# Recurrent steps set between attention steps, and a shorter program for the experts' third blocks

## The chip, the cores and the metric

One NeuronCore of a Trainium2 chip runs one layer of a hybrid decoder in a single launch. The measure is the device time of that core in microseconds, lower is better. Engines are named as in the profile: PE (TensorE, matrix products), DVE (VectorE), ACT (ScalarE), POOL (GpSimd) and SP (SyncE, which here issues transfers).

## What is computed

The layer projects 2048 tokens of width 1024 once, and four mixers work on the columns: RWKV (A), gated linear attention (B, "GLA"), mLSTM (C) and latent softmax attention (D). Their outputs are projected and normalized; then a mixture of 32 experts, two for each token, and a gated side input follow.

```python
u  = x @ w_in[i]
ua, ub, uc, ud = split_last(u, (D_IN_A, D_IN_B, D_IN_C, D_IN_D))
ya = rwkv7_group(ua, ...)
yb = gla_group(ub, ...)          # chunked scan: scores in the chunk, plus a carried state
yc = mlstm_group(uc, ...)        # chunked scan with a carried maximum
yd = mla_group(ud, cos, sin, ...)
mix = jnp.concatenate([ya, yb, yc, yd], axis=-1) @ w_out[i]
x   = layer_norm(DN_ALPHA * x + mix, ln1_g[i], ln1_b[i], LN_EPS)
ffn = hier_moe(x, w_rg, b_rg, w_re, b_re, w_gate, w_up, w_down)
ple = jax.nn.sigmoid(x @ ple_w_gate[i] + ple_b_gate[i]) * (p[i] @ ple_w[i])
x   = layer_norm(DN_ALPHA * x + ffn + ple, ln2_g[i], ln2_b[i], LN_EPS)
# an expert: (silu(xb @ w_gate[e]) * (xb @ w_up[e])) @ w_down[e]
```

## The kernel before

The program runs in stages: projections with the RWKV mixer (to about 1060 us), the attention stage (to about 1590), output projection, side input and routing (to about 2016), the experts (to about 3010) and the last normalization.

**Attention stage.** Tokens go in four quarters of 512. Softmax attention is a generator, `d`, of small steps: `mla_attend` makes the scores of one block of 128 keys against 512 queries (three matmuls at L1242 into an `sbank`), their exponential on ACT (`mla_pt`), its sum on POOL or DVE (`mla_acc`, L1248) and now and then the product with the values (`obank`, L1222). Steps of the query maximum are mixed in: a matmul into an `mbank` (L1205), then a reduction `mla_m` on DVE (L1209). The keys and queries are split in a high and a low part, the low ones by DVE at L52 (`mla_kl`, `mla_ql`).

GLA (`gla`) and mLSTM (`mlstm`) go through a quarter in four tiles of 128 tokens. A GLA tile copies the query into the zeroed `gl_qz` (L743), multiplies for scores into a `gbank` (L745), masks them on DVE into `g_am` (L747), transposes the key into another `gbank` (L749, `g_kk`), forms the state's new part (L752), and adds the products of state and scores (`acc`, L264 and L268), copied to `g_yt` by ACT (L767). An mLSTM tile works likewise with `cbank`s and ends in `c_yt` (L967) and the state's update (L975). After the fourth tile of a quarter, `head_norm` (L284 to L294) normalizes the whole quarter, 128 x 1024 elements for each of the two, on DVE, ACT and POOL, and the gate is applied (L776, L981).

The banks (`gbank`, `cbank`, `mbank`, `sbank`, `obank`) are accumulators from small pools: a matmul into a bank waits until the last reader of that buffer is done. A scheduler reorders the emitted instructions on each engine, so the order of an engine is near that of the code but not the same; it is shown below where it matters. In `layer` the loop over 16 tiles emits eight steps of attention (`MLA_RATE`), then a GLA tile and an mLSTM tile.

**Experts.** For each expert the tokens come in blocks of 128, the first always (`moe_gu` 48 matmuls, `moe_dn` 24), the second if the expert has more than 128 tokens, the third if it has more than 256. Counts are known at run time only, so the second and third block stand under an `If` of the program. Each number is split in high and low part, and a product is three passes: high x high, high x low, low x high. For a block of at most 64 tokens `sized` (L1911) picks a shorter program in which the low parts of the tokens stand in the second half of the block's 128 columns ("spread"), so that two passes do. `third(e)` (L1926 to L1943) holds, in one If (L1929), the third block's down product of expert e (L1931) and the gate and up products of expert e+1 (L1936), each with both programs: 4 transposes and 24 + 16 matmuls, 8 transposes and 48 + 32 matmuls, 132 in all. The If of the second block's gate and up products is at L1969, with 48 + 32 matmuls. Products of high and low rows are added by `fold` (gate and up) and in `moe_y` with the mask `half`, L1843 (down).

Of the kernel before, what the change touches and what calls it, by code (L numbers as in the profile page):

```python
# [8 lines left out]
F32 = mybir.dt.float32  # L9
# [21 lines left out]
class Layer:  # L31
# [701 lines left out]
    def gla(self, q):  # L733
        nc, e, s1 = self.nc, self.e, self.s1
        qt, kt, v, gate = self.gin.pop(q)
        fin = self.gfin[:, q]
        yt = e.tile([128, 4, 256], F32, name="g_yt", bufs=1)
        for tt in range(4):
            c = slice(tt * 128, tt * 128 + 128)
            qz = self.qz[tt % 2]  # L740
            for hd in range(4):
                g = slice(32 * hd, 32 * hd + 32)
                nc.vector.tensor_copy(qz[g, hd, :], qt[g, c])  # L743
            p = self.gbank()
            nc.tensor.matmul(p, kt[:, c], qz, start=True, stop=True)  # L745
            st = e.tile([128, 4, 128], F32, name="g_am")
            nc.vector.tensor_mul(st, p.rearrange("p (h i) -> p h i", h=4), self.incl[:, None, :].to_broadcast([128, 4, 128]))  # L747
            p = self.gbank()
            nc.tensor.transpose(p[:, 0:128], kt[:, c], self.ident)  # L749
            kk = e.tile([128, 128], F32, name="g_kk")  # L750
            nc.scalar.copy(kk, p[:, 0:128])
            nc.tensor.matmul(p[:, 256:512], kk, v[:, tt, :], start=True, stop=True)  # L752
            po = self.gbank()
            first = q == 0 and tt == 0
            if not first:
                x = e.tile([128, 256], F32, name="gl_x", bufs=1)
                nc.vector.scalar_tensor_tensor(x, self.gxe, fin[:, tt:tt + 1], self.gbd.rearrange("p h c -> p (h c)"),
                                               op0=OP.mult, op1=OP.mult)
                nc.tensor.matmul(po[:, 0:256], qt[:, c], x, start=True, stop=False, skip_group_check=True)
                nc.vector.tensor_add(self.gxe, p[:, 256:512], x)  # L760
            else:
                self.zero_bank(po, 256)
                nc.vector.tensor_copy(self.gxe, p[:, 256:512])
            for hd in range(4):
                g = slice(64 * hd, 64 * hd + 64)
                self.acc(po[:, g], st[:, hd, :], v[:, tt, g])
            nc.scalar.copy(yt[:, tt, :], po[:, 0:256])  # L767
            if tt == self.LOAD_AT and q < 3:
                self.gla_load(q + 1)
            yield  # L770
        self.gla_out(q, yt, gate)
# [152 lines left out]
    def mlstm(self, q):  # L924
# [3 lines left out]
        for tt in range(4):  # L928
# [9 lines left out]
            for hd in range(4):  # L938
                nc.scalar.activation(w[:, hd], p[:, hd * 128:hd * 128 + 128], AF.Exp, bias=self.mgt[:, 0, 16 * hd + ch:16 * hd + ch + 1])
            pr = e.tile([128, 4, 128], F32, name="c_am")  # L940
            for s in range(2):
                g = slice(64 * s, 64 * s + 64)
                p = self.cbank()
                for hp in range(2):
                    nc.tensor.matmul(p[:, hp * 128:hp * 128 + 128], qk[2 + hp][g, c], qk[hp][g, c], start=True, stop=True)
                nc.vector.scalar_tensor_tensor(pr[:, s::2, :], p[:, 0:256].rearrange("p (a i) -> p a i", a=2), 0.125, w[:, s::2, :],
                                               op0=OP.mult, op1=OP.mult)
            p = self.cbank()
            for hp in range(2):
# [3 lines left out]
                                           g4(2)[:, :, None].to_broadcast([128, 4, 64]), op0=OP.mult, op1=OP.mult)  # L953
            pn = self.cbank()
# [12 lines left out]
            nc.vector.tensor_mul(yt[:, tt, :].rearrange("p (h c) -> p h c", h=4), hn[:, :, 0:64], dn[:, :, None].to_broadcast([128, 4, 64]))  # L967
            pk = self.cbank()
# [10 lines left out]
            yield  # L979
# [713 lines left out]
    def lists(self, lt):  # L1693
# [24 lines left out]

        def pick(j, i):

            nc.vector.tensor_copy(u, p[:, j * 128:j * 128 + n])
            nc.vector.tensor_sub(u, u, p[:, i * 128:i * 128 + n])
            nc.vector.tensor_mul(u, u, half)
            nc.vector.tensor_add(u, u, p[:, i * 128:i * 128 + n])
# [63 lines left out]
    def passes(self, x, wh, wl, k, half):  # L1788
# [4 lines left out]
        return (x[0][:, k], wh), (x[0][:, k], wl), (x[1][:, k], wh)  # L1793

# [57 lines left out]
    def moe(self, G0=(), x0=None, experts=32):  # L1852
# [74 lines left out]
        def third(e):  # L1927

            with tc.If(cnt[e + 1, "four"] > 256):  # L1929
                if e >= 0:  # L1930
                    with tc.If(one(e) > 256):  # L1931
                        h = self.moe_ht(hx, spread=True)
                        sized(e, 2, lambda s: self.moe_dn(h, DW[e], yb, half=s))
                        self.moe_put(self.moe_y(yb, half(e, 2)), put(e, 2))
                if e + 1 < experts:
                    with tc.If(one(e + 1) > 256):  # L1936
                        x = self.turned(X[2], spread=True)
                        sized(e + 1, 2, lambda s: self.moe_gu(x, GW[e + 1], yb, half=s))
# [248 lines left out]
def layer(ctx, tc, I, out):  # L2187
# [3 lines left out]
    with ExitStack() as c:  # L2191
# [35 lines left out]
        for i in range(16):  # L2227
            if i >= L.MLA_WAIT:
                for _ in range(L.MLA_RATE):
                    next(d, None)  # L2230
            next(g)
            next(m)
# [51 lines left out]
```

## Time and profile before

| | us |
|---|---|
| median of 3 runs (3108.67 to 3115.36) | 3111.82 |
| the profiled execution | 3114.34 |
| its span, first to last instruction | 3112.4 |
| PE busy in it | 2830.1 |
| DVE busy | 1949.2 |
| ACT busy | 1224.5 |
| POOL busy | 892.6 |

The granted TensorE clock has a mean of 0.941 over the span. A windows row gives for each engine the busy time and, in brackets, the number of instructions; PEclk is the mean granted clock of that stretch as a share of full speed. A wait is put down to the instruction that released it last.

### The profile page before, as it was taken

The page shows a single profiled execution, that of the slowest core. Times are in us where ns is not written, and L with a number is a line of the kernel's source. Part 1 is how long each engine was busy: PE and PEld are TensorE (multiplying, and loading weights), DVE is VectorE, ACT ScalarE, POOL GpSimd, SP SyncE. Part 2 cuts the span into 40 slices and gives each one's busy share as a digit, 9 for nine tenths or more (in the row PEclk, how much of TensorE's full clock was granted, in tenths as well). Part 3 has the DMA queues.
Part 4 walks back from the last instruction along what each step waited for, and adds up shares of the span by engine and source line. Part 5 has one row for each costly group of instructions (what it writes and reads, how often), then busy time and mean ns, then how long its engine had stood idle before and what let it go on. Part 6 is the DMA issues. An engine that isn't in the chain of part 4 may idle for free. (4 is left out here: it accounts for less than half of the span.)

```text
span 3112.4 us, 42881 instructions
## 1 busy us (share of the span) xinstructions
PE 2830.1 (91%) x15420; PEld 2239.0 (72%) x15421; DVE 1949.2 (63%) x4094; ACT 1224.5 (39%) x2001; POOL 892.6 (29%) x552
## 2 busy tenths in 40 slices
PE   8999999998999899989999999888889988998883
PEld 6888888777877665655567799777667766776662
DVE  6366543566555466667656644676667756666869
ACT  4223232222124332323320122265666756666752
POOL 1000100111010023334331201445454545554525
PEclk9999999999998898979999999999999989999996
DMA  6332143111134522110143412377687867777873
GB/s 186 109 93 75 47 130 93 52 57 56 53 80 136 177 58 70 47 39 18 55 158 136 147 62 75 105 277 257 203 271 242 274 206 233 268 260 224 284 247 137
DMA packets 287055, 443.19 MB, mean 142 GB/s; under 512 B 84088, under 2 KB 152040, under 8 KB 286760
## 3 DMA queue, kind: packets, MB, share of 16 engines
q1 hardware_dynamic: 272200, 397.78, 38.3%
q0 software_dynamic: 14560, 41.47, 5.4%
q8 instruction: 185, 3.03, 0.4%
q14 instruction: 110, 0.90, 0.1%
HBM read 350.52 MB, written 96.50 MB: 144 GB/s over the span
## 5 line engine op out<-in xcount | busy, mean ns | idle before, releaser
L1802 PE MATMUL m_g<-m_g,xhl 128*128 128x512 f32 x2032 | 514.4, 401 | 15.1 <-PEq L1929 9.4
L1802 PEld LDWEIGHTS m_g<-m_g,xhl 128*128 128x128 f32 x2032 | 372.6, 190 | 105.8 <-issue 31.2
L1773 DVE TENSOR_TENSOR m_g<-m_raw,m_g 128x1024 fp32r<-128x1024 f32 x188 | 260.9, 1413 | 131.9 <-ACT m_g L1772 112.5
L1772 ACT CAST m_g<-m_raw 128x1024 fp32r<-128x1024 f32 x252 | 255.3, 1057 | 123.4 <-PEq L1929 110.5
L1834 PE MATMUL m_y<-m_dh,m_h 128*128 128x512 f32 x672 | 239.6, 421 | 24.9 <-PEq L1929 6.5
L59 PE MATMUL pbank<-xh,wh 128*128 128x512 f32 x544 | 220.6, 405 | 10.6 <-DVE us L209 7.7
L60 PE MATMUL pbank<-xl,wh 128*128 128x512 f32 x544 | 219.4, 403 | 0.0
L61 PE MATMUL pbank<-xh,wl 128*128 128x512 f32 x544 | 218.6, 402 | 0.1
L51 ACT CAST xhl<-bank 128x512 fp32r<-128x512 f32 x204 | 118.3, 607 | 251.5 <-PE bank L1350 250.2
L1773 POOL TENSOR_TENSOR m_g<-m_raw,m_g 128x1024 fp32r<-128x1024 f32 x64 | 183.6, 2951 | 88.1 <-ACT m_g L1772 48.3
L1408 PE MATMUL wide<-wt,xhl 128*128 128x512 f32 x768 | 183.5, 398 | 3.6 <-ACT xhl L51 3.6
L1773 POOL TENSOR_TENSOR m_dl<-m_raw,m_dh 128x1024 fp32r<-128x1024 f32 x64 | 178.0, 2806 | 20.6 <-ACT m_dh L1772 20.3
L1834 PEld LDWEIGHTS m_y<-m_dh,m_h 128*128 128x128 f32 x672 | 137.3, 204 | 59.7 <-issue 9.4
L1408 PEld LDWEIGHTS wide<-wt,xhl 128*128 128x128 f32 x768 | 144.1, 189 | 39.8 <-ACT xhl L51 7.3
L1248 POOL TENSOR_TENSOR mla_acc<-mla_acc,mla_pt 128x512 f32<-128x512 f32 (+3 forms) x112 | 137.7, 1230 | 115.0 <-ACT mla_pt L1246 94.5
L52 DVE TENSOR_TENSOR xhl<-bank,xhl 128x512 fp32r<-128x512 f32 x204 | 136.5, 685 | 50.4 <-ACT xhl L51 48.6
L1848 POOL DMA_INDIRECT accd<-m_y,m_put x47 | 92.4, 1967 | 255.1 <-ACT m_y L1841 160.6
L1246 ACT ACTIVATE mla_pt<-sbank 128x512 f32<-128x512 f32 (+3 forms) x160 | 85.0, 532 | 200.6 <-PE sbank L1242 116.8
L1834 PE MATMUL m_y<-m_dl,m_h 128*128 128x512 f32 x376 | 155.8, 414 | 0.0
L1588 PE MATMUL gate<-wt,xhl 128*128 128x354 f32 (+1 forms) x864 | 150.2, 331 | 0.3 <-ACT xhl L51 0.2
L59 PE MATMUL pbank<-wh,xh 128*128 128x256 f32 x512 | 150.3, 294 | 0.0
L60 PE MATMUL pbank<-wl,xh 128*128 128x256 f32 x512 | 150.0, 293 | 0.0
(635 smaller groups left out, 6306.2 us busy)
## 6 DMA issues: line engine op xcount, KB each, us to landing
m_raw<-in_moe_w_down SPq DMA_DIRECT2D x64, 1024.0 KB
m_raw<-in_moe_w_gate SPq DMA_DIRECT2D x126, 512.0 KB
m_raw<-in_moe_w_up SPq DMA_DIRECT2D x126, 512.0 KB
wraw<-in_w_in SPq DMA_DIRECT2D x80, 256.0 KB
o_x<-in_x SPq DMA_DIRECT2D x16, 512.0 KB
x1d<-m_g SPq DMA_DIRECT2D x16, 512.0 KB
accd<-wide SPq DMA_DIRECT2D x16, 512.0 KB
m_raw<-accd SPq DMA_DIRECT2D x7, 1024.0 KB
```

The costliest lines, as they stand in the source:

```text
L51: nc.scalar.copy(hi, src)
L52: (eng and nc.gpsimd or nc.vector).tensor_sub(lo, src, hi.bitcast(F32))
L59: nc.tensor.matmul(out, lh, rh, start=start, stop=False)
L60: nc.tensor.matmul(out, lh, rl, start=False, stop=False)
L61: nc.tensor.matmul(out, ll, rh, start=False, stop=stop)
L1248: (nc.vector if kt in self.SUMS else nc.gpsimd).tensor_add(acc[:, c0 * 128:512], acc[:, c0 * 128:512], pt[:, 0:n])
L1408: nc.tensor.matmul(p[:, j], a[:, k], W[k][bb][:, j * 512:j * 512 + 512], start=k == 0 and i == 0, stop=k == 7 and i == 2)
L1588: nc.tensor.matmul(p[:, 0:n], a[:, k], b[:, o:o + n], start=k == 0 and i == 0, stop=k == 7 and i == 2)
L1772: self.nc.scalar.copy(h[:, i], raw[:, i])
L1773: lo_eng.tensor_sub(l[:, i], raw[:, i], h[:, i].bitcast(F32))
L1802: self.mark["pe"] = self.nc.tensor.matmul(banks[:, j], a, b[:, k % 2, j * 512:j * 512 + 512], start=k == 0 and i == 0, stop=k == 7 and i = ...
L1834: self.nc.tensor.matmul(p[:, j], a, b[:, k % 2, j * 512:j * 512 + 512], start=k == 0 and i == 0, stop=k == 3 and i == len(ps) - 1)
```

## The change

In the attention stage, `gla` and `mlstm` now yield after each small piece, seven times for a GLA tile and eight for an mLSTM tile, and say "tile" at its end. The loop in `layer` takes one step of attention, then one piece of GLA and one of mLSTM, eight times for a tile; what is left of the tile then follows. The addition to the GLA state (`gl_xe`) stands ahead of the product with the old state, and the bank of that product is taken later.

```diff
         for i in range(16):
-            if i >= L.MLA_WAIT:
-                for _ in range(L.MLA_RATE):
-                    next(d, None)
-            next(g)
-            next(m)
+            rest = [g, m]
+            for k in range(L.MLA_RATE):
+                next(d, None)
+                for x in list(rest):
+                    if next(x) == "tile":
+                        rest.remove(x)
+            for x in rest:
+                while next(x) != "tile":
+                    pass
```

In `gla` the piece ends are these (those of `mlstm` are of the same kind: after the weights `ml_w`, after each half of `c_am`, two after `ml_kw`, two after `c_yt`, and "tile"):

```diff
                 nc.vector.tensor_copy(qz[g, hd, :], qt[g, c])
+            yield
             p = self.gbank()
             nc.tensor.matmul(p, kt[:, c], qz, start=True, stop=True)
             st = e.tile([128, 4, 128], F32, name="g_am")
             nc.vector.tensor_mul(st, p.rearrange("p (h i) -> p h i", h=4), self.incl[:, None, :].to_broadcast([128, 4, 128]))
+            yield
+            yield
             p = self.gbank()
             nc.tensor.transpose(p[:, 0:128], kt[:, c], self.ident)
             kk = e.tile([128, 128], F32, name="g_kk")
             nc.scalar.copy(kk, p[:, 0:128])
+            yield
             nc.tensor.matmul(p[:, 256:512], kk, v[:, tt, :], start=True, stop=True)
-            po = self.gbank()
...
+                nc.vector.tensor_add(self.gxe, p[:, 256:512], x)
+                yield
+                yield
+                po = self.gbank()
                 nc.tensor.matmul(po[:, 0:256], qt[:, c], x, start=True, stop=False, skip_group_check=True)
-                nc.vector.tensor_add(self.gxe, p[:, 256:512], x)
...
-            yield
+            yield "tile"
```

In the experts' third blocks one program takes the place of two. `beside_lo` puts the low parts of the first 64 columns beside the high ones, times the mask `half` (one where the block has at most 64 tokens, else zero); `lean` then makes two passes, and a third, low x high, under an If of its own when there are more than 64. The bodies hold 4 + 16 + 8 and 8 + 32 + 16 matmuls, 84 in all. Where blocks are listed, `pick` takes the mask `plain`, which is one for third blocks.

```diff
+    def beside_lo(self, x, m):
+        hi, lo = x[0], x[1]
+        self.nc.vector.scalar_tensor_tensor(hi[:, :, 64:128], lo[:, :, 0:64].bitcast(F32), m, hi[:, :, 64:128].bitcast(F32),
+                                            op0=OP.mult, op1=OP.add)
+
+    def lean(self, x, W, p, n, full):
+        for j in range(2):
+            c = slice(j * 512, j * 512 + 512)
+            for k in range(n):
+                wh, wl = W[k // 2]
+                for i, w in enumerate((wh, wl)):
+                    self.nc.tensor.matmul(p[:, j], x[0][:, k], w[:, k % 2, c], start=k == 0 and i == 0, stop=k == n - 1 and i == 1)
+        with self.tc.If(full):
+            for j in range(2):
+                for k in range(n):
+                    self.acc(p[:, j], x[1][:, k], W[k // 2][0][:, k % 2, j * 512:j * 512 + 512], stop=k == n - 1)
...
                     with tc.If(one(e) > 256):
-                        h = self.moe_ht(hx, spread=True)
-                        sized(e, 2, lambda s: self.moe_dn(h, DW[e], yb, half=s))
+                        h = self.moe_ht(hx)
+                        self.beside_lo(h, half(e, 2))
+                        self.lean(h, DW[e], yb, 4, cnt[e, "pe"] > 320)
...
                     with tc.If(one(e + 1) > 256):
-                        x = self.turned(X[2], spread=True)
-                        sized(e + 1, 2, lambda s: self.moe_gu(x, GW[e + 1], yb, half=s))
+                        x = self.turned(X[2])
+                        self.beside_lo(x, half(e + 1, 2))
+                        self.lean(x, GW[e + 1], yb, 8, cnt[e + 1, "pe"] > 320)
```

Line numbers move: L745 becomes L746, L749 becomes L752, L747 becomes L748, L1242 becomes L1257, L1205 becomes L1220, L1929 becomes L1968.

PE at the end of the attention stage's second quarter, before, from the last attention product to the GLA transpose and a little beyond:

```order
L1222 MATMUL obank<-mla_pt,mla_v_8192 64x384
L745 MATMUL gbank<-gl_qz_8062,g_k 128x512
L933 LDWEIGHTS identb
L933 MATMUL cbank<-negm,identb 128x512
L268 MATMUL cbank<-ml_nmu,ident 128x128 x3
L749 MATMUL gbank<-ident,g_k 128x128
L268 MATMUL cbank<-ml_nmu,ident 128x128
L945 MATMUL cbank<-c_a,c_k 128x128
L752 MATMUL gbank<-g_v,g_kk 128x256
```

PE at the same place now, from the GLA score product on:

```order
L746 MATMUL gbank<-gl_qz_8061,g_k 128x512
L1220 MATMUL mbank<-mla_kh_8188,mla_qh 128x512
L955 MATMUL cbank<-c_a,c_k 128x128
L955 MATMUL cbank<-c_q,c_z 128x128
L1257 MATMUL sbank<-mla_qh,mla_kh_8189 128x512
L1257 MATMUL sbank<-mla_ql,mla_kh_8189 128x512
L1257 MATMUL sbank<-mla_qh,mla_kl_8191 128x512
L1220 MATMUL mbank<-mla_kh_8188,mla_qh 128x256
L268 LDWEIGHTS identb
L268 MATMUL mbank<-negq,identb 128x128
L955 MATMUL cbank<-c_a,c_k 128x128
L1220 MATMUL mbank<-mla_kh_8188,mla_qh 128x512
```

Between the score product and the transpose (L749, now L752, which stands 17 rows after L746) there are now scores and query maxima of two attention steps.

DVE at the end of the first quarter, before, from the first sum of mLSTM's `head_norm` to the mask product:

```order
L284 TENSOR_REDUCE hn_stc_th<-c_yt 128x16
L52 TENSOR_TENSOR mla_kl_8190<-mla_x,mla_kh_8188 64x512
L285 TENSOR_SCALAR hn_stc_th<-hn_stc_th 128x16
L286 TENSOR_TENSOR c_yt<-c_yt,hn_stc_th 128x1024
L52 TENSOR_TENSOR mla_kl_8190<-mla_x,mla_kh_8188 64x512
L52 TENSOR_TENSOR mla_ql<-mla_x,mla_qh 96x512
L747 TENSOR_TENSOR g_am<-gbank,incl 128x512
```

DVE at the same place now:

```order
L284 TENSOR_REDUCE hn_stc_th<-c_yt 128x16
L289 TENSOR_REDUCE hn_stg_th<-g_th 128x16
L990 SCALAR_TENSOR_TENSOR ml_st_8075<-ml_st_8075,ml_dc,cbank 64x65 x2
L990 SCALAR_TENSOR_TENSOR ml_st_8076<-ml_st_8076,ml_dc,cbank 64x65 x2
L290 TENSOR_SCALAR hn_stg_th<-hn_stg_th 128x16
L285 TENSOR_SCALAR hn_stc_th<-hn_stc_th 128x16
L52 TENSOR_TENSOR mla_kl_8190<-mla_x,mla_kh_8188 64x512
L68 TENSOR_SCALAR rs_thg_th<-hn_stg_th 128x16
L286 TENSOR_TENSOR c_yt<-c_yt,hn_stc_th 128x1024
L69 TENSOR_SCALAR hn_rsg_th<-rs_thg_th 128x16
L71 TENSOR_TENSOR rs_thg_th<-hn_rsg_th 128x16
L72 SCALAR_TENSOR_TENSOR rs_thg_th<-rs_thg_th,hn_stg_th 128x16
```

The mask product (now L748) follows right behind; `head_norm` of GLA now runs among that of mLSTM instead of ahead of it, two of the three splits at L52 stand behind the mask product, and the next two reductions of the query maximum come 44 rows after it.

PE in the gate and up part of the third blocks' If, before:

```order
L1943 TENSOR_LOAD m_tcnt
L1936 COMPARE_AND_BRANCH
L1350 MATMUL bank<-ident,m_xg_18063 128x128 x8
L1911 COMPARE_AND_BRANCH
L1802 MATMUL m_y<-m_g,xhl 128x512 x48
L1911 UNCONDITIONAL_BRANCH
L1802 MATMUL m_y<-m_g,xhl 128x512 x32
L1911 UNCONDITIONAL_BRANCH
L1936 UNCONDITIONAL_BRANCH x2
L1929 UNCONDITIONAL_BRANCH
```

PE in the same part now:

```order
L1984 TENSOR_LOAD m_tcnt
L1976 COMPARE_AND_BRANCH
L1365 MATMUL bank<-ident,m_xg_18066 128x128 x8
L1828 MATMUL m_y<-m_g,xhl 128x512 x32
L1829 COMPARE_AND_BRANCH
L268 MATMUL m_y<-m_g,xhl 128x512 x16
L1829 UNCONDITIONAL_BRANCH x2
L1976 UNCONDITIONAL_BRANCH x2
L1968 UNCONDITIONAL_BRANCH
```

The choice between 48 and 32 matmuls has become 32 always and 16 more under an If.

## Rows read from the trace of the kernel before

**Rows 1.** The page: engines' busy time, share and instructions.

```profile
PE 2830.1 (91%) x15420; PEld 2239.0 (72%) x15421; DVE 1949.2 (63%) x4094; ACT 1224.5 (39%) x2001; POOL 892.6 (29%) x552
```

**Rows 2.** Windows: stretch, its length, each engine's busy us, clock, DMA, GB/s.

```profile
1060.00:1510.00 450.00, 423.60 (x2083) 269.98 (x2081) 289.93 (x696) 139.41 (x295) 143.06 (x118) 0.90 0.20 57
1100.00:1190.00 90.00, 88.82 (x465) 54.16 (x466) 61.31 (x156) 32.70 (x64) 31.79 (x30) 1.00 0.17 49
1330.00:1340.00 10.00, 2.44 (x9) 1.27 (x9) 9.76 (x18) 1.56 (x4) 6.82 (x4) 0.67 0.41 124
2016.00:3010.00 994.00, 881.63 (x3998) 704.00 (x3997) 687.99 (x733) 633.32 (x852) 498.46 (x220) 0.96 0.75 250
```

**Rows 3.** PE's waits from 1060 to 1510: releaser, us in total, times, longest.

```profile
PE gbank L749 <- DVE g_am L747: 12.8, 4, 6.7
...
PE gbank L745 <- ACT g_yt L767: 2.9, 2, 2.4
PE mbank L1205 <- DVE mla_m L1209: 2.4, 6, 0.9
```

**Rows 4.** PE's timeline, 1328 to 1342: start, us, instruction, count, idle before.

```profile
1331.51 1.13 PE L745 MATMUL gbank<-gl_qz,g_k 128*128 128x512 f32 x2 [2.35 <-ACT g_yt L767]
...
1332.79 1.17 PE L268 MATMUL cbank<-ml_nmu,ident 64*128 64x128 f32 x6
1340.64 0.48 PE L749 MATMUL gbank<-ident,g_k 128*128 128x128 f32 x1 [6.68 <-DVE g_am L747]
```

**Rows 5.** DVE's timeline, 1316 to 1342.

```profile
1319.13 0.21 DVE L743 COPY gl_qz<-g_q 32x128 f32<-32x128 f32 x1
...
1323.09 2.35 DVE L743 COPY gl_qz<-g_q 32x128 f32<-32x128 f32 x1
...
1339.89 0.69 DVE L747 TENSOR_TENSOR g_am<-gbank,incl 128x512 f32<-128x512 f32 x1
```

**Rows 6.** Windows of two stretches at the low clock after quarter ends.

```profile
1200.20:1224.10 23.90, 23.04 (x78) 17.30 (x78) 11.20 (x38) 2.96 (x8) 3.73 (x4) 0.50 0.12 29
1333.30:1370.80 37.50, 30.82 (x105) 21.77 (x105) 20.11 (x41) 5.31 (x13) 10.28 (x8) 0.50 0.17 48
```

**Rows 7.** PE's waits in the experts' stage, 2000 to 2960.

```profile
PE bank L1350 <- PEq L1929: 20.4, 9, 6.3
PE bank L1350 <- DVE m_h L52: 11.3, 4, 4.2
...
PE m_g L1802 <- PEq L1929: 9.1, 13, 2.0
PE m_y L1834 <- PEq L1929: 6.5, 4, 3.3
```

**Rows 8.** Branch lines on PE's queue: count, ns min/median/max, first and last start.

```profile
L1929 PEldq EVENT_SEMAPHORE  x58: 51/51/51, 2024.5 to 2998.1; - x58
L1929 PEldq COMPARE_BRANCH  x33: 70/442/7024, 2024.0 to 2996.0; - x33
L1929 PEldq COMPARE_BRANCH  x1: 2962/2962/2962, 2133.7 to 2133.7; - x1
L1929 PEldq COMPARE_BRANCH  x1: 3550/3550/3550, 2942.1 to 2942.1; - x1
L1969 PEldq COMPARE_BRANCH  x32: 70/216/365, 2019.6 to 2962.4; - x32
L1969 PEldq EVENT_SEMAPHORE  x19: 51/51/51, 2023.4 to 2966.3; - x19
```

**Rows 9.** Windows of the first low-clock stretch after a long skip, and the sum of seven.

```profile
2278.80:2285.60 6.80, 5.67 (x18) 4.85 (x19) 4.43 (x7) 5.83 (x8) 0.99 (x1) 0.50 0.63 222
...
sum 37.40, PE 31.31 PEld 26.88 DVE 29.44 ACT 32.93 POOL 16.22; mean PE 4.47 PEld 3.84 DVE 4.21 ACT 4.70 POOL 2.32
```

**Rows 10.** Groups in the experts' stage: count, busy us, mean ns of one, idle before.

```profile
L1843 DVE SCALAR_TENSOR_TENSOR m_y<-m_y,m_half 64x512 f32<-64x512 f32 x66 | 49.6, 752 | 27.4 <-ACT m_y L1841 25.8
...
L1802 PE MATMUL m_y<-m_g,xhl 128*128 128x512 f32 x64 | 17.0, 426 | 2.2 <-DVE xhl L52 2.2
```

More of the change, by code (lines that the diff above doesn't have):

```diff
@@ L758, in gla @@
                                                op0=OP.mult, op1=OP.mult)
+                nc.vector.tensor_add(self.gxe, p[:, 256:512], x)
+                yield
+                yield
+                po = self.gbank()
                 nc.tensor.matmul(po[:, 0:256], qt[:, c], x, start=True, stop=False, skip_group_check=True)
-                nc.vector.tensor_add(self.gxe, p[:, 256:512], x)
             else:
+                nc.vector.tensor_copy(self.gxe, p[:, 256:512])
+                yield
+                yield
+                po = self.gbank()
                 self.zero_bank(po, 256)
-                nc.vector.tensor_copy(self.gxe, p[:, 256:512])
             for hd in range(4):
@@ L939, in mlstm @@
                 nc.scalar.activation(w[:, hd], p[:, hd * 128:hd * 128 + 128], AF.Exp, bias=self.mgt[:, 0, 16 * hd + ch:16 * hd + ch + 1])
+            yield
             pr = e.tile([128, 4, 128], F32, name="c_am")
@@ L947, in mlstm @@
                                                op0=OP.mult, op1=OP.mult)
+                yield
             p = self.cbank()
@@ L953, in mlstm @@
                                            g4(2)[:, :, None].to_broadcast([128, 4, 64]), op0=OP.mult, op1=OP.mult)
+            yield
+            yield
             pn = self.cbank()
@@ L967, in mlstm @@
             nc.vector.tensor_mul(yt[:, tt, :].rearrange("p (h c) -> p h c", h=4), hn[:, :, 0:64], dn[:, :, None].to_broadcast([128, 4, 64]))
+            yield
+            yield
             pk = self.cbank()
@@ L978, in mlstm @@
                 self.mlstm_load(q + 1)
-            yield
+            yield "tile"
         self.head_norm(yt, 4, 1e-5, True, self.ml_g, "c_th")
@@ L1717, in lists @@
             nc.vector.tensor_scalar(v[:, b], self.base, 128.0 * b + 64, None, op0=OP.is_le)
+        plain = tl([128, n], F32, "m_plain")
+        nc.vector.tensor_copy(plain, half)
+        for b in range(2, self.NB):
+            nc.vector.memset(plain.rearrange("p (e b) -> p b e", e=32)[:, b], 1.0)
         def pick(j, i):
@@ L1722, in pick @@
             nc.vector.tensor_sub(u, u, p[:, i * 128:i * 128 + n])
-            nc.vector.tensor_mul(u, u, half)
+            nc.vector.tensor_mul(u, u, plain)
             nc.vector.tensor_add(u, u, p[:, i * 128:i * 128 + n])
```

## Prediction

> **What bounds the kernel now.** I read the page's engine table first: TensorE (PE) is busy 2830.1 of 3112.4 us, the next engine, VectorE (DVE), 1949.2 [rows 1]. A gain can only come from PE's idle time or from stretches at a low granted clock. Then the windows by stage. In the attention stage, 1060 to 1510 us, PE is busy 423.6 of 450 us and the mean granted clock is 0.90; a quiet piece of it (1100 to 1190) has PE busy 88.8 of 90 us at 1.00, so the loss lies in a few places. In the experts' stage PE is busy 882 of 994 us at 0.96 [rows 2]. The change touches these two stages, and for each I read PE's waits by releaser, then the timeline at the worst place.
>
> Attention: PE's longest named wait is the transpose at L749, 12.8 us in four waits, one of 6.7, put down to DVE's mask multiplication g_am at L747. L745, which waits for the copy g_yt of the tile before, has another 2.9 [rows 3]. On PE's timeline L745 runs at 1331.51, short matmuls follow to about 1334, and L749 starts at 1340.64 after 6.68 us of nothing [rows 4]. L749 needs no result of L747 as data; it needs a gbank, and of the few banks one is free only when g_am has read it. DVE's timeline says why g_am is late: it is not waiting but works through the quarter's end, head_norm of both recurrences and the split of the next keys, and these are stretched while POOL works beside it. The same L743 copy takes 0.21 us at 1319 and 2.35 us at 1323, and g_am itself starts only at 1339.89 [rows 5]. In the window of that stall DVE is busy 9.76 of 10 us, PE 2.44 [rows 2]. [...] With the 12.8 + 2.9 us of waits the quarter ends cost 42.6 us.
>
> Experts: PE's waits on its own sequencer at L1929, the If around the third blocks, are 20.4 + 9.1 + 6.5 = 36.0 us [rows 7]. That branch runs 33 times on PE's queue, median 442 ns, longest 7024; its 58 semaphore records, two for each skip, say that 29 of the runs skip the body [rows 8]. 11 of the skips took over 1.7 us, 41 us together (the first and the last of them stand in [rows 8]); the other 18 lie near the median, some 8 us. So about 28 of the 36 us of PE's waits are the long ones. After seven of them the clock is at 0.50, for 37.4 us together [rows 9], which costs at most half, 18.7. The price of the long skips is 28 + 18.7, about 46 us. What tells a long skip from a short one? Each matmul has its own weight load (15420 against 15421 instructions [rows 1]), so the body of L1929, 132 matmuls in its four programs, is 264 instructions and some branches. The If at L1969 guards the two programs of the second block, 80 matmuls or 160 instructions. It is skipped 19 times of 32, and its longest run is 365 ns [rows 8]. A jump over 160 instructions has never stalled here; one over 264 has, 11 times in 29.
>
> **The change, part by part.** (1) Attention order. Before, eight attention steps were emitted and then a whole tile of both recurrences; after, each step is followed by a seventh or an eighth of a tile. No instruction of PE goes or comes; the rows move. At the second quarter's end PE had seven short matmuls, about 1.5 us, between L745 and L749 [rows 4]; after, the same two (now L746 and L752) have score matmuls of two attention steps between them, 16 rows. At the rate of the quiet stretch these are 3.7 to 4 us of work. g_am may be late by so much more before PE stops. DVE's rows move as well: I added the durations of DVE's rows from the tile's last c_yt to g_am, in the new order, with their unstretched times. At the second quarter's end that is 9.7 us against 10.9 us of PE work until the transpose that needs it: about balanced. At the first quarter's end g_am comes 7.9 us after c_yt, but the next query-max reduction (mla_m) only some 26 us of DVE work after it, since now all of head_norm stands in front, while PE is at the matmul that needs that bank after 24. Two to three us are missing there, and as much at the next matmuls of the kind. Stretched as in [rows 5], DVE is 4 or 5 us later still. From this I put the loss that remains at 12 us at the first end (5 to 20, the upper end being the 18 it costs now), at 5 at the second (1 to 20), clock included. 42.6 - 17 is 25.6; I take **25 us** (3 to 37).
>
> [...]
>
> (2) Third blocks. The body of L1929 goes from 132 to 84 matmuls: 168 instructions and some 20 others, near the 160 that never stalled. Against a full cure: in the code only six matmuls stand between the If at L1969 and the one at L1929, so that often both are skipped in a row, 160 + 264 instructions before, 160 + 168 after. Read by the jump alone all 11 go; read by the sum of the two, 328 on a line from 160 (none) to 424 (11) leaves 7. I take 60% avoided, 28 us. Of that not all is kept: in the stage DMA is at 0.75 and DVE busy 688 of 994 us [rows 2], and a PE that no longer stops comes earlier to the waits for the next weights. I keep 0.6 of it, between 1 (PE alone bounds) and 0.3: 17 us.
>
> (3) What is added. Third blocks run for two experts, as 64 matmuls into m_y show for 2 x 32 [rows 10], so four bodies: each now has one more DVE instruction, beside_lo, between the splitting and the first matmul. Its nearest row is L1843, 752 ns [rows 10]; with the hand-over 1 to 1.5 us each, **4 us** in all (3 to 11, if each waits as long as PE's mean wait for m_h, 11.3 / 4 [rows 7]). The number of matmuls that run in these bodies is the same, 32 and 16, since both blocks were small. The mask plain and its use in pick are two small DVE rows in a stretch in which DVE idles: nothing. So the experts give 17 - 4 = **13 us** (-5 to 24).
>
> The sum goes against the profiled run, 3114.3 us: 3114.3 - 25 - 13 = 3076. The median of the three runs is 2.5 us lower, so **3074 us**, 1.2% faster.
>
> **The rivals.** *The waits only move (3099).* DVE has the same rows to do, stretched by the same GpSimd work; PE stops at L752 or at the query-max banks instead, as long as now, and the clock falls as now. Only the 13 us of the experts come: 3099. For it: DVE is busy 9.8 of 10 us in the stall [rows 2]. Against it: PE stops for lack of 6.7 us in a stage where most banks have slack, and after the change it has other work in between.
>
> *Slower (3130).* One mechanism: at each of three quarter ends the query-max reductions now stand behind 26 us of DVE rows. If these are stretched by a third, PE is starved for some 8 us at each, not in one gap but in three or four, with the clock low meanwhile and beyond. At 8 us and a clock loss of 15 (as after the second end now, half of 30.8 [rows 6]) three ends cost 69 us where 43 are lost: 26 more. With half of the experts' gain left, 3111.8 + 26 - 7, some 3130. It decides when the first reduction after a quarter end comes more than 5 us after PE is ready for it.
>
> *The branch keeps its stalls (3087).* The skip still leads too far, or what PE no longer waits for it waits for in the weights: only attention's 25 us, 3087. For it: the chain of two skips, and DMA's 0.75.
>
> *The branch loses all its long skips (3063).* By jump length alone all 46 us go; with 0.6 kept and 4 us paid that is 24 instead of 13, so 3063. [...]
>
> **How the numbers follow.** Chances: the forecast 0.40, all skips cured 0.14, waits only move 0.16, branch keeps its stalls 0.12, slower 0.11, and both gains absent (3112, nothing moved that PE waits for) 0.07. A measurement of this kernel tells some 0.2%, 6 us, from no change. The first four are faster by more, but the third and fourth reach over that border in a tenth of their cases: faster 0.77, same 0.11, slower 0.12. For the range: the forecast's own bounds are 3112 - 37 - 24 = 3051 and 3112 - 3 + 5 = 3114. Beyond an upper end at 3110 lie the slower case, the unchanged one and little else, near 2 in 10; the lower end I put at 3046, for a full cure of the skips of which more than 0.6 is kept.
>
> **What would show it.** Right, if the waits of L752 on g_am fall below 5 us in all, the clock at 1333 to 1371 stays at 1.00, and the If of the third blocks has at most five runs over 1.5 us. Wrong in its first part, if PE's waits for mla_m grow from 2.4 us [rows 3] to over 10, or the half-clock stretches stay as long. Wrong in its second, if long skips of that If stay near 11, or if the waits move to the splits m_h and xhl or to the weights.

## The result, and the profile after

The changed kernel took 3083.65 us (median of 4 runs, 3078.95 to 3088.71), the kernel before 3113.59 us beside it: ratio 0.990, 95% interval 0.9875 to 0.9925, some 30 us less. Two later sets gave 0.9914 (0.9883 to 0.9944) and 0.9901 (0.9867 to 0.9935). The forecast was 3074 us, 38 less.

The page of the profiled run after (its span is 3077.1 us): engines' busy time, and the queue that carries instructions (185 packets before).

```profile
PE 2825.4 (92%) x15420; PEld 2226.6 (72%) x15421; DVE 1968.1 (64%) x4100; ACT 1224.0 (40%) x2001; POOL 892.3 (29%) x552
...
q8 instruction: 172, 2.82, 0.4%
```

PE runs as many instructions as in [rows 1], and its busy time is the same within 5 us; so nearly all of the gain is idle time. PE's waits in the attention stage, 1060 to 1500 us (releaser: us in total, times, longest), against [rows 3]:

```profile
PE cbank L985 <- DVE ml_hn L974: 4.1, 3, 3.3
...
PE gbank L766 <- DVE gl_xe L762: 3.3, 4, 1.2
PE mbank L1220 <- DVE mla_m L1224: 1.8, 4, 1.0
PE gbank L752 <- DVE g_am L748: 1.6, 2, 0.8
...
PE gbank L746 <- ACT g_yt L776: 0.6, 1, 0.6
```

The waits on g_am fell from 12.8 to 1.6 us, those on g_yt from 2.9 to 0.6, and mla_m did not grow. New are 3.3 us of the mLSTM product at L985 near 1205 us, behind the same burst of DVE work at the first quarter's end, and the waits on gl_xe grew from 1.0 us to 3.8 (L766 and L264 together). The clock did not follow. Windows after (columns as in [rows 2]): the whole stage, and three stretches at the low level.

```profile
1060.00:1495.00 435.00, 416.64 (x2097) 264.96 (x2096) 298.00 (x709) 140.69 (x298) 143.21 (x121) 0.91 0.20 59
...
1165.00:1175.20 10.20, 10.20 (x28) 6.08 (x28) 4.17 (x10) 3.33 (x8) 2.52 (x2) 0.50 0.06 13
1209.30:1233.20 23.90, 23.90 (x76) 15.82 (x76) 13.03 (x33) 5.12 (x13) 5.81 (x4) 0.50 0.29 90
...
1342.40:1356.10 13.70, 13.70 (x41) 8.05 (x41) 6.17 (x15) 3.62 (x10) 2.01 (x3) 0.50 0.05 11
```

From the first c_yt to the last mla_yt, which bounds the part of the stage where the mixers meet, it is 482.7 us before and 465.4 after. The clock is at 0.50 for 78.3 us of it before and for 71.6 after; the stretch of 37.5 us in [rows 6] is gone, but 10.2, 3.4, 13.7 and 6.8 us have come at other places, at 1165, 1295, 1342 and 1421 (10.2 us at 1496 have their like before, at 1517.7). The windows of this part, before and then after, tell what the gain is made of:

```profile
1096.30:1579.00 482.70, 457.14 (x2206) 283.45 (x2206) 315.92 (x723) 156.06 (x319) 188.09 (x151) 0.92 0.17 51
```

```profile
1095.60:1561.00 465.40, 450.42 (x2210) 277.42 (x2209) 317.79 (x722) 155.97 (x320) 183.52 (x151) 0.92 0.18 53
```

And the sums of the stretches at 0.50 in it, before and then after:

```profile
sum 78.30, PE 70.43 PEld 47.23 DVE 38.67 ACT 10.66 POOL 23.87; mean PE 14.09 PEld 9.45 DVE 7.73 ACT 2.13 POOL 4.77
```

```profile
sum 71.60, PE 71.22 PEld 43.49 DVE 35.94 ACT 21.42 POOL 15.59; mean PE 10.17 PEld 6.21 DVE 5.13 ACT 3.06 POOL 2.23
```

PE's idle time fell from 25.6 to 15.0 us, which is 10.6 of the 17.3 us. Its busy time at the low level did not fall, 70.4 us before and 71.2 after. The other 6.7 us are busy time, which is shorter by the records for as many matmuls (within 4); why, stays open.

PE's waits in the experts' stage (1990 to 2940 us), against [rows 7]:

```profile
PE m_g L1841 <- PEq L1968: 7.6, 12, 2.1
...
PE m_y L1828 <- DVE m_h L1818: 5.7, 2, 3.6
...
PE m_y L1828 <- DVE xhl L1818: 5.0, 2, 2.5
...
PE bank L1365 <- PEq L1968: 3.7, 8, 0.5
...
PE m_y L1873 <- PEq L1968: 2.4, 2, 1.9
```

And the third blocks' If on PE's queue (columns as in [rows 8]):

```profile
L1968 PEldq COMPARE_BRANCH  x33: 70/231/3341, 2009.0 to 2960.2; - x33
```

The waits on the branch fell from 36.0 to 13.7 us, and 3 runs of it last over 1.5 us, where 11 did. From its first run to the end of its last there are 972.2 us before and 951.4 after. The four iterations in which a third block runs cost 165.6 us before and 175.2 after, from start to start of the If: each waits for beside_lo (L1818, in the rows above). So in this pair of profiles 30.4 us were won in the rest of the stage, where the If is skipped, and 9.6 given back where it is not.

### The profile page after: what moved, and what is told of

Same layout as the page of the kernel before. It is cut to its first block, busy times and chain, and to the rows that moved or that the text cites. A ratio compares the mean times of both kernels' runs of the same rounds, so it can differ in the third digit from the quotient of the medians.

```text
span 3077.1 us, 42863 instructions
## 1 busy us (share of the span) xinstructions
PE 2825.4 (92%) x15420; PEld 2226.6 (72%) x15421; DVE 1968.1 (64%) x4100; ACT 1224.0 (40%) x2001; POOL 892.3 (29%) x552
## 5 line engine op out<-in xcount | busy, mean ns | idle before, releaser
L1873 PE MATMUL m_y<-m_dh,m_h 128*128 128x512 f32 x656 | 226.5, 410 | 23.4 <-ACT m_y L1880 6.7
L1873 PEld LDWEIGHTS m_y<-m_dh,m_h 128*128 128x128 f32 x656 | 129.7, 198 | 55.9 <-ACT m_y L1880 8.9
L52 DVE TENSOR_TENSOR xhl<-bank,xhl 128x512 fp32r<-128x512 f32 x204 | 136.3, 684 | 45.2 <-ACT xhl L51 43.2
L61 PE MATMUL pbank<-wh,xl 128*128 128x256 f32 x512 | 150.3, 294 | 0.0
```

Source lines behind the costliest of these rows:

```text
L52: (eng and nc.gpsimd or nc.vector).tensor_sub(lo, src, hi.bitcast(F32))
L61: nc.tensor.matmul(out, ll, rh, start=False, stop=stop)
L1873: self.nc.tensor.matmul(p[:, j], a, b[:, k % 2, j * 512:j * 512 + 512], start=k == 0 and i == 0, stop=k == 3 and i == len(ps) - 1)
```

## The experiments

All ratios are to the kernel before, run beside it. The order alone, the first run of the shorter third blocks, the padded body and the body of 60 were timed in one set, in which the change itself was not run.

| kernel | ratio | 95% interval |
|---|---|---|
| order alone | 0.9927 | 0.9907 to 0.9948 |
| shorter third blocks alone | 0.9990 | 0.9966 to 1.0014 |
| the same again | 0.9983 | 0.9970 to 0.9996 |
| change, third blocks' body padded | 0.9979 | 0.9961 to 0.9997 |
| change, body of 60 matmuls | 0.9929 | 0.9903 to 0.9954 |
| change, late end of attention blocks | 0.9896 | 0.9870 to 0.9922 |
| late end and normalization in steps | 0.9891 | 0.9870 to 0.9913 |
| the same again | 0.9906 | 0.9869 to 0.9943 |

Two more kernels leave a part of the computation out and were timed once each: the one with a short second block took 3109.47 us (the kernel before beside it 3115.67), the one without the quarters' normalization 3093.93 us (3119.94).

### One part at a time

The order alone takes the hunks of `gla`, `mlstm` and `layer`:

> The kernel before with the attention part of the change alone. In the profiles of before and after the experts' stage begins 15.0 us earlier (first run of the third blocks' If at 2024.0 and 2009.0). If the two parts are independent, this kernel has that gain alone: ratio 0.995 to before, some 3098 us. By the prediction's 25 us it would be 0.992. If the order's gain were only a shift that the experts' stage swallows, 1.000.

The shorter third blocks alone take the others:

> The kernel before with the shorter third blocks alone. From the first to the last run of that If there are 972.0 us in before and 951.2 in after, so 20.8 us are expected: ratio 0.9935, some 3093 us, and 2 to 5 skips of more than 1.5 us in place of 11. By the prediction's 13 us it would be 0.996. If the short program only shifts what PE waits for, 1.000.

The order gave 0.9927, some 23 us (16 to 29): the forecast's 25, more than the 15 that I had read from the two profiles. Its own profile has 477.9 us from first c_yt to last mla_yt, with 105.8 at the low clock, against 465.4 and 71.6 in the change: single executions of one order differ so much, and nearly all of it is clock. The shorter third blocks gave nothing sure, though their own profile has 953.9 us for the stretch that is 972.2 in before. So both were run again, the change beside the one part:

> The changed kernel once more, beside the others of this set. By its own measurement 0.990 to before. If the two parts simply add as the first set timed them (order 0.9927, shorter third blocks 0.999), 0.992.

> The kernel before with the shorter third blocks alone, again, since its time (0.999, 0.9966 to 1.0014) and its stage (953.9 us against 972.2 before) disagree. If the stage tells the truth, 0.993 to 0.995; if the skips that it saves are given back elsewhere, 0.999 again, and the attention stage, which it leaves alone, ends at the same time as in before.

The second time it was 0.9983, 1 to 9 us less than before, with 959.7 us in the stretch; the change beside it had 0.9914. By time, 23 + 5 make the 27 to 31 us of the change: within the intervals the parts add up, and the third blocks are the small one.

### How long a jump stalls

Padding: matmuls that never run, in the body of the If.

```diff
                         self.lean(x, GW[e + 1], yb, 8, cnt[e + 1, "pe"] > 320)
+                        with tc.If(cnt[e + 1, "pe"] > 2040):
+                            self.moe_gu(x, GW[e + 1], yb)
```

> The changed kernel with 48 matmuls that never run (under an If that asks for more than 2040 tokens) put into the third blocks' body, so that the skip is as long as before, 132 matmuls. If the length of the skip makes the stalls, about 11 skips over 1.5 us come back and the time is 20 to 25 us above the changed kernel, some 3105. If the leaner running program or the changed place in the program made the gain, the skips stay at 3 or so and the time near 3084.

Shortening: `lean` without the pass under `If(full)`.

> The changed kernel without the third pass for third blocks of more than 64 tokens (left out; no such block comes in this data), so that the skip is over 60 matmuls. By the length theory the last three long skips go, 5 us at most: 3079 to 3084. If what is left has another cause, 3 long skips remain and the time is that of the changed kernel.

The If on PE's queue in the padded kernel, then in the one of 60 matmuls:

```profile
L1968 PEldq COMPARE_BRANCH  x33: 70/447/6596, 2022.8 to 3002.1; - x33
```

```profile
L1964 PEldq COMPARE_BRANCH  x33: 70/335/3052, 2018.6 to 2973.1; - x33
```

With 132 matmuls in the body, 12 runs last over 1.5 us; with 60, 3, as with 84. But for one more If in the bodies, the instructions that run are the same in the padded kernel and the change. So in these kernels the number of long skips goes with the length of the code jumped over, 12 of 29 against 3. Between the two of this set, 0.9979 and 0.9929, lie 15.6 us by time.

Not all of the padded kernel's time is skips. The order alone has a body of 132 too, and 10 long skips, and yet it took 15.4 us less in the same set (0.9927, with intervals that do not touch). By the profiles the difference lies where a third block runs: the four iterations take 161.3 us in the order alone and 176.1 in the padded kernel. So in this set shortening the body wins some 15 us by time, and the new program with beside_lo costs about as much: with 60 matmuls the time is that of the order alone, 0.9929 against 0.9927.

The other candidate was the sum of the two jumps that stand six matmuls apart:

```diff
             with tc.If(cnt[e, "pe"] > 128):
-                sized(e, 1, lambda s: self.moe_gu(x1, GW[e], b1, half=s))
+                self.moe_gu(x1, GW[e], b1, half=True)
```

> The kernel before with one program in place of two for the second block's gate and up products (always the shorter one of 32 matmuls; for five experts with over 64 tokens there the third pass is left out), so that the skip at the second block's If is over 32 matmuls and not 80, while the third blocks keep their 132. Both skips in a row are then 164 matmuls, as in the changed kernel (80 + 84). If the sum of two skips makes the long ones, 3 to 5 skips over 1.5 us are left; if the third blocks' own jump does, about 11 stay. Five experts run 16 matmuls less each, some 18 us.

```profile
L1929 PEldq COMPARE_BRANCH  x33: 70/1522/6483, 2028.1 to 2990.7; - x33
```

That is the If of this kernel: 17 runs over 1.5 us, more than in before, with the sum of both jumps as in the change. The sum does not rule it; that theory falls. Nor does the jump's own length alone, since that is the 132 matmuls of before. Why 17 skips are long here, behind a jump of 32 matmuls, and 11 in before, behind one of 80, stays open.

### What a quarter's end costs

The kernel before without the two `head_norm` calls of GLA and mLSTM:

> The kernel before without the normalization of GLA's and mLSTM's quarters (head_norm is left out there; its sums, rsqrt and scalings are missing). If DVE's work at a quarter's end holds TensorE, the waits of the transpose on g_am (12.8 us) and the low-clock stretches at 1200 and 1333 us go, and the attention stage is 35 to 43 us shorter. If something else holds it (the splits, the banks), most of them stay.

A window of that kernel over both quarter ends, and PE's wait on g_am in 1060 to 1490:

```profile
1100.00:1480.00 380.00, 375.52 (x1985) 235.95 (x1985) 227.96 (x569) 123.16 (x270) 128.72 (x112) 1.00 0.17 50
```

```profile
PE gbank L749 <- DVE g_am L747: 2.1, 5, 0.8
```

The clock is at 1.00 throughout this window, the wait on g_am is 2.1 us, and the stretch from first c_yt to last mla_yt is 439.0 us, 43.7 less than in before. The normalization is the cause; it runs on DVE, ACT and POOL, and DVE's share was not taken out alone. Its price is near that of the prediction (42.6). The prediction's way of pricing comes out as well. The window from first c_yt to last mla_yt:

```profile
1103.80:1542.80 439.00, 431.61 (x2211) 267.03 (x2209) 251.87 (x599) 148.86 (x312) 161.91 (x143) 0.98 0.19 56
```

PE's idle time in it is 7.4 us, 18.2 less than before, and its busy time at the low level 16.6 us, 53.8 less, half of which is 26.9; together 45.1. The change, at 465.4, has 17.3 of the 43.7.

The gain of this stage did not all arrive at the end. The span of this one execution is 3091.8 us, 20.6 less than before: the first c_yt came 7.5 us later, and the part with the third blocks' If took 982.9 us against 972.2.

### Why the clock stayed low

On PE's timeline of the changed kernel there is no stall in the 8 us before the fall at 1342.4; there is an attention block's end (L1279, L1280: 64 columns and 1), with the mLSTM's small matmuls before it and 1.2 us of matmuls of up to 512 columns behind it:

```profile
1336.70 0.71 PE L985 MATMUL cbank<-c_v,ml_kw 128*128 128x130 f32 x4
...
1338.59 0.71 PE L268 MATMUL cbank<-ml_nmu,ident 64*128 64x128 f32 x4
1339.22 0.43 PE L1279 MATMUL sbank<-twice,mla_pt 128*128 128x64 f32 x2
1339.49 0.33 PE L1280 MATMUL sbank<-ones,mla_acc 128*128 128x1 f32 x2
...
1340.84 0.33 PE L1280 MATMUL sbank<-ones,mla_acc 128*128 128x1 f32 x2
```

In the window of 1338.0 to 1342.4 PE is busy 4.40 of 4.40 us:

```profile
1338.00:1342.40 4.40, 4.40 (x28) 3.44 (x29) 2.21 (x7) 0.59 (x1) 0.00 (x0) 1.00 0.33 91
```

The same ends stand before the falls at 1165, 1295 and 1421; the last has two stalls in the 6 us before it, of 0.57 and 0.44 us. Counted from the first c_yt, the four recur within 4 us in the profiles of both repeats of the change. In the order alone, the padded kernel and the one of 60, which have the same attention stage, the last three recur within 7 us; the one at 1165 is missing in the kernel of 60. To test whether the ends make the falls, they were put off:

```diff
             nc.scalar.activation(pt[:, 0:n], p[:, 0:n], AF.Exp)
+            if kt == 1:
+                self.mla_finish()
+                acc = l.tile([128, 512], F32, name="mla_acc", bufs=1)
...
         nc.scalar.copy(ot, po)
-        p = self.sbank()
-        for tt in range(4):
...
+        self.ended = hd, q, ot, acc
```

> The changed kernel with the eight small matmuls that end an attention block (64 columns and 1) issued behind the second step of the next block, not right at the end, where the narrow scores of the diagonal and the recurrent steps' small matmuls stand too. The same work. If the granted clock falls because small matmuls stand together, the low stretches that follow such ends without a stall (1165, 1295, 1342 and 1421 us, 34 us together) go or shrink, and the time falls by 10 to 17 us against the changed kernel. If only waits of TensorE lower the clock, those stretches stay or move at random, and the time is the same.

Windows of this kernel over the four places, and over the first quarter's end:

```profile
1289.00:1299.00 10.00, 10.00 (x59) 6.82 (x55) 9.73 (x24) 5.37 (x12) 1.86 (x3) 1.00 0.59 157
1340.00:1355.00 15.00, 15.00 (x96) 11.07 (x94) 9.48 (x26) 4.75 (x12) 2.75 (x4) 1.00 0.05 10
...
1420.00:1430.00 10.00, 10.00 (x51) 5.55 (x48) 6.68 (x20) 2.87 (x6) 2.53 (x2) 1.00 0.00 0
1160.00:1178.00 18.00, 18.00 (x107) 12.05 (x105) 11.82 (x34) 6.88 (x15) 3.97 (x5) 1.00 0.12 29
1207.00:1232.00 25.00, 23.67 (x76) 15.41 (x76) 14.15 (x35) 4.51 (x12) 6.08 (x6) 0.52 0.36 108
```

All four stretches are gone; the one behind the stall at the first quarter's end is there as before. But 13.7 us at the low clock have come at 1457, behind an end that now meets another group of small matmuls; 10.2 stand at 1491, where the change has as much at 1496, and 10.2 at 1526, where it has 3.4 at 1534. In sum 61.9 us in place of 71.6, and 459.1 us in place of 465.4; the order alone and the kernel of 60, which share one attention stage, have 105.8 and 64.8, so a sum says little. By time 0.9896 against 0.9914 for the change beside it, 6 us less, with intervals that overlap. So where the ends stand moves the falls; that it is the small matmuls' standing together which lowers the clock is not shown, and the next kernel speaks against it as the whole cause.

The last step was to cut `head_norm` into steps of the same kind, one at every second attention step, with the late ends kept:

> The changed kernel with the late end of attention blocks (as in the run before) and with the quarters' normalization cut into steps too, one at every second attention step, over two tiles; the outputs of a quarter get a second buffer. If DVE's burst at a quarter's end is what still starves TensorE (4.5 us of gaps near 1200 us and 23.9 us at the low clock after them), these go: 12 to 16 us less than with the late end alone, ratio 0.985. If the burst is only spread into more places where TensorE waits, the attention stage stays at 459 us from first c_yt to last mla_yt.

PE's waits in that kernel, 1090 to 1560 us:

```profile
PE mbank L1238 <- DVE mla_m L1242: 6.8, 5, 2.9
PE gbank L759 <- DVE g_am L755: 4.6, 2, 4.2
...
PE cbank L998 <- DVE ml_hn L987: 1.7, 1, 1.7
```

The wait on ml_hn went from 3.3 to 1.7 us; in its place came waits on the query maxima and on g_am at the second end: 17.7 us of gaps in the stretch against 12.6 with the late end alone. The stretch is 455.1 us long, 4 less, not 12 to 16.

This kernel has the late ends too, so its clock bears on the question above. In the third quarter, the kernel with the late end alone runs these rows, and its clock stays at 1.00 through them and to 1430:

```profile
1411.19 1.16 PE L268 MATMUL cbank<-ml_nmu,ident 64*128 64x128 f32 x8
...
1413.08 0.33 PE L1290 MATMUL sbank<-twice,mla_pt 128*128 128x64 f32 x2
```

```profile
1406.00:1417.00 11.00, 9.43 (x55) 6.26 (x54) 10.09 (x26) 3.43 (x9) 6.89 (x4) 1.00 0.17 56
```

The kernel with the normalization in steps has the same PE rows in the same order there, from the mLSTM's product (L985, here L998) on, with no stall between them, and its clock falls behind them:

```profile
1409.37 1.16 PE L268 MATMUL cbank<-ml_nmu,ident 64*128 64x128 f32 x8
...
1411.25 0.33 PE L1308 MATMUL sbank<-twice,mla_pt 128*128 128x64 f32 x2
```

```profile
1406.80:1413.40 6.60, 6.54 (x43) 5.06 (x42) 6.55 (x10) 2.81 (x7) 5.78 (x4) 1.00 0.01 2
1413.40:1427.10 13.70, 12.16 (x29) 6.44 (x30) 9.77 (x25) 1.19 (x2) 4.90 (x3) 0.50 0.27 86
```

One row of matmuls, two outcomes. The small matmuls do not tell them apart, and the only stall in these windows, 1.57 us just ahead of the rows, belongs to the kernel whose clock did not fall. The rows further ahead differ. What makes the clock fall there stays open.

By time the kernel gave 0.9891. It was run again beside the change:

> The changed kernel a third time, as the partner of the next: 0.990 to 0.992 to before.

> The kernel with late ends and normalization in steps, again, beside the changed kernel on the same chip. Its attention stage was 455.1 us from the first c_yt to the last mla_yt, against 465.4 and 467.5 in the changed kernel: if that holds without a profile, 10 to 12 us less than the changed kernel, ratio 0.987 to 0.988. If it was the spread of single executions, the two are equal.

0.9906 against 0.9901: equal. (The two profiles of this set are not compared by stage; the second had a mean clock of 0.893, and 0.95 in quiet stretches too.) No version here is shown to beat the change.

## Why the prediction was right, point by point

**What bounds the kernel.** Right: idle time and low clock at the quarter ends and at one branch. The price of the quarter ends, 42.6 us, is 15.7 of waits [rows 3] and 26.9, half of PE's busy time in the two windows of [rows 6]; it is 43.7 by the run without the normalization, which takes the work of all the ends away, on all three engines. No run shows the 26.9 by itself: it takes PE's work at 0.50 to need twice its time. In the trace of before, matmuls of 512 columns at L1242 start 0.43 us apart at 0.50 (1358.01 and 1358.44) and 0.24 apart at 1.00 (1372.51 and 1372.75), a little less than twice.

**The order, 25 us.** Right in size, 23 by time (17 in the profile), wrong in its make-up. The waits went as said: g_am from 12.8 to 1.6 us, under the 5 named. The balance at the second end held. At the first end the forecast had the query maxima late by two or three us; late was ml_hn, by 3.3, for the reason given: small DVE instructions stretched while POOL works. DVE's timeline after, near that stall, and POOL's:

```profile
1201.69 2.12 DVE L71 TENSOR_TENSOR rs_thc_th<-hn_rsc_th 128x16 f32<-128x16 f32 x1
...
1204.08 2.20 DVE L72 SCALAR_TENSOR_TENSOR rs_thc_th<-rs_thc_th,hn_stc_th 128x16 f32<-128x16 f32 x1
...
1207.62 0.42 DVE L974 TENSOR_TENSOR ml_hn<-cbank,ml_gt 128x260 f32<-128x260 f32 x1
```

```profile
1201.43 2.34 POOL L294 TENSOR_TENSOR g_yt<-g_yt,gl_g 128x1024 f32<-128x1024 f32 x1 [1.70 <-DVE hn_rsc_th L73]
1203.85 2.41 POOL L785 TENSOR_TENSOR g_yt<-g_yt,g_gate 128x1024 f32<-128x1024 f32 x1
```

Each of the two stretched rows begins after a POOL instruction has begun and ends within 0.04 us of it (at 1203.81 against 1203.77, and 1206.28 against 1206.26).

The step that failed is the clock: I counted its loss as something that hangs on a stall and goes with it, and wrote that 1333 to 1371 would be at 1.00. 13.7 us of it were at 0.50, and the stage's sum at the low level went from 78.3 only to 71.6 us. PE's busy time in it, half of which the forecast counts as the loss, is 70.4 us before and 71.2 after: the clock gave nothing, and the 17 are 10.6 of idle time and 6.7 of shorter busy time. By the forecast's own reckoning 16.5 us remain at the first end (waits of 1.2 and 3.3, half of 23.9) and 8.8 at the second (waits of 2.0, half of 13.7), 25 where it had 17. That makes the 17 us of gain which the two profiles show; the 23 by time is nearer to 25 than this account is, and with an interval of 16 to 29 some of that can be luck.

With POOL idle, from 1207.47 to 1210.20, the same two operations take 0.18 us (L71 at 1207.53) and 0.17 (L72 at 1207.96). No run here took POOL's work alone away, so that POOL's work is what stretches them is read from these rows and not shown by a run.

**The third blocks, 13 us.** The two terms were 17 won and 4 paid. Won: 30 us in the profile, 15.6 by time (padded against 60 matmuls). Paid: 9.6 us in the pair of profiles, and 14.8 between the order alone and the padded kernel, not 4; the hand-over to beside_lo waits for both halves of the split, and the upper bound of 11 was the better price. The net is 5 by time (4.7 and 5.9 in two sets; 1.4 between the order alone and the kernel of 60). This is the term that was mis-sized, and it makes most of the difference between 3074 and 3083.65. Why the profiles show twice as much for the skips as the times do is open. It is not the spread of one pair: the part with the If takes 965.0 to 982.9 us in the four profiles with a body of 132 and an unchanged second block, and 950.1 to 959.7 in the nine with 84 or 60. The profiled executions themselves lean that way: that of the order alone took 3107.62 us, the most of its six (median 3097.82), those of the shorter third blocks 3105.81 and 3099.16 (medians 3116.46 and 3114.08).

**Length or sum of jumps.** I took 60% between the two; the runs decide against the sum and for the jump's own length (12 against 3), though not for it alone (17 at the same length with a short jump ahead). Not a full cure, either: 3 of 29 stay with 84 matmuls and 3 with 60. What PE's queue does in a long skip, no run here shows.

**The rivals.** "The waits only move" held for a part: DVE's burst still stops PE at the first end (3.3 us on ml_hn). "Slower" fell: the query maxima waited 1.8 us, not 8 at each end. "The branch keeps its stalls" fell by the profile, and the full cure did too. Of the signs that the forecast named, the waits on g_am (1.6 us) and the long skips (3) came out; the clock at 1333 to 1371 did not, and waits did move to the splits m_h and xhl, 10.7 us at beside_lo. By its own rule its chances of being faster add up to 0.79, not 0.77.

## What to carry to other kernels

Where one engine does a burst for a stage's end while another waits for a bank, put independent work of the waiting engine between the two matmuls (here the waits on g_am fell from 12.8 to 1.6 us); to price the burst, run the kernel without it once. Do not book the low clock as a part of the stall before it (PE's busy time at 0.50 stayed, 70.4 us before and 71.2 after): look what stands on the matrix engine when the clock falls, and check a guess on it in more than one kernel, since one row of matmuls here went both ways. Branch bodies that mostly are skipped can cost by their length in code (over 132 matmuls 11 of 29 skips were long before, over 84 it was 3 after), so a shorter body that does the same work can pay; count what it adds on the runs that do take it, and settle the gain by time, as the profiles here showed twice as much.

## What the runs showed of the hardware

In the changed kernel the granted clock fell from 1.00 to 0.50 with PE busy 4.40 of 4.40 us by its records, after 2.6 us of matmuls of 1 to 128 columns and 1.2 us of matmuls of up to 512. With the end of 64 columns and 1 put off it stayed at 1.00 there. Behind one other row of matmuls, the same in two kernels, it stayed at 1.00 in one and was at 0.50 for 13.7 us in the other. Two DVE operations that take 0.18 and 0.17 us with POOL idle took 2.12 and 2.20 beside POOL instructions and ended within 0.04 us of them. And a branch of PE's queue over 132 matmuls took 1.5 to 7.0 us in 10 to 12 of its 29 skips, over 84 or 60 in 2 to 5, and over 132 behind a jump of 32 in 17.
